# A decoder layer on one core: the attention gate's columns moved ahead of the recurrent branch's columns, softmax normalisation moved from ScalarE to VectorE, and two small reorderings at the start

## The chip, the cores and the metric

The kernel runs on one core of a Trainium2 chip. The metric is device time of one execution in microseconds (us). Before the change it is 998.0 us, the median of three runs that span 997.78 to 998.13 us.

A core has five engines that run side by side, each with its own queue of instructions in program order: TensorE (PE in the profile, with PEld for its weight loads), VectorE (DVE), ScalarE (ACT), GpSimd (POOL) and SyncE (SP), which here only issues DMA transfers. An instruction that waits for data holds back everything behind it on its engine.

## The reference

One layer of a hybrid decoder is computed for 512 prompt positions and for 8 samples of 4 positions each (544 columns in all, model width 1024):

```python
def _mixer(h, ...):
    proj = h @ w_in
    xr, q, k, v, g = jnp.split(proj, [c0, c1, c2, c3], axis=-1)
    g_lru, g_attn = jnp.split(g, 2, axis=-1)
    xc, conv_state = _causal_dwconv(xr, lru_conv_prev, conv_w, conv_b)      # width 4
    lru_out, h_last = _rg_lru(xc, lru_h0, wr, br, wi, bi, lam, pos0)        # gates from xc, then a scan
    ...                                                                     # windowed attention, softmax with a sink
    merged = jax.nn.sigmoid(g_lru) * (lru_out @ w_lru_o) + jax.nn.sigmoid(g_attn) * (attn @ w_attn_o)
    return merged @ w_out, ...
```

and then `x + RMSNorm(m)` and a feed-forward part with a width-3 convolution. The softmax is `p = exp(s - m)`, `p / (sum(p) + exp(sink - m))`. All inputs and outputs are float32.

## The kernel before, in words

**Layout.** Activations lie transposed: 128 channels on the partitions, the 544 positions along the free axis. They are worked in two halves, `a = 0` (256 columns) and `a = 1` (288 columns: 256 prompt and 32 sample positions). Every float32 operand is split into a high and a low part (`H` and `L`), and each product is three matmuls: high by high, high by low, low by high. Splitting a weight is a ScalarE copy (line 281, `wh`) and a VectorE subtraction (line 288, `wl`); splitting an activation is the same pair at lines 700 and 703, 817 and 818, 839 and 840, 957 and 958.

**Steps and ticks.** The mixer is a series of steps (`step`, line 342). A step multiplies one 128-column block of a weight by one half of the activations: 24 matmuls into one PSUM tile, of which there are three (`PM`). After step s comes tick s+1 (`tick`, line 194), which writes further work into the queues of the engines, always in this order: the high splits of the weight unit that is claimed (ScalarE); the list `late`, which holds the treatment of the result of step s-1 (from tick 8 on it comes before the side work); the side work that is due (`sides`); the list `after`; the low splits of the claimed unit (VectorE); the list `last`. One weight unit (half of a column block) is claimed at each tick, two columns ahead (`look=2`), or one ahead (`look=1`) from tick 51 on, when the gate weights `wg` hold a third of the split buffers.

**Order of the steps** (`order`, line 234; loops at lines 1062 to 1108). Steps 0 to 9 make five column blocks of q, k and v, first halves and then second halves. Steps 10 to 23 make the other seven q, k, v blocks. Steps 24 to 39 make the eight blocks of the recurrent branch (`xr`, columns 0 to 7), steps 40 to 55 the eight blocks of the attention gate (`ga`, columns 28 to 35), steps 56 to 71 the attention's output projection (`ao`), steps 72 to 87 the recurrent gate (`gl`), and then follow the projections `lo` and `out` and the feed-forward part.

**Treatment of a result.** A gate block costs VectorE one multiplication per half by the norm factors `rep` (`scaled`, line 705). A recurrent block costs one for the first half and two for the second (`xr_done`, lines 934, 938, 939), then a ScalarE pass that starts the convolution (line 942) and, from the list `after`, three VectorE passes over all 568 columns (`xr_taps`, line 951).

**Side work**, by the tick at which it is due. Sixteen attention units (a pair of heads, 128 queries) start at the ticks in `ATTN`; each takes one tick per stage: scores `psc` on TensorE; softmax on VectorE and exponentials on ScalarE (`softmax_a`); sum, reciprocal and normalisation (`softmax_b`, line 775, where the normalisation is a ScalarE multiplication put into `after`, line 779); transposes `pt`; split of the transposes; the product with v, `pvp`; and, for every second unit, the split of the result (`aH`, `aL`, one pair of instructions per head that take turns on one PSUM tile). The last units start at ticks 36, 39, 42 and 45. The samples' attention (`sample_attn`, line 859) comes in two groups. Group 0 has scores `pss` at tick 42, softmax at 43, normalisation at 44, transposes `pst` at 45, at tick 46 a VectorE copy of them (`spt`, lines 901 and 902) and at once the product `pso` that reads the copy, then copy, transpose and, at tick 49, eight pairs of tiny splits that take turns on ScalarE and VectorE (lines 920 and 921). Group 1 is five ticks later (`spt` and `pso` at tick 51, the eight pairs at 54). The recurrent gates (`gates`, line 955) of blocks 0 to 3 start at ticks 51, 53, 55 and 57: split of `xc` (`xcH` on ScalarE, `xcL` on VectorE); a tick later 12 matmuls `pg`; a tick later four sigmoids on ScalarE; a tick later a VectorE multiplication (line 979). Their exponentials follow from tick 58. The attention gate's own sigmoids (line 1085) run at ticks 52 to 58.

**The start.** The first column block is made while x is still being transposed. `turn_a(0)` and `turn_a(1)` (line 465) transpose the first and the second half of the channels of positions 0 to 255; ScalarE and VectorE split them (`hsplit`, line 449: `hH`, `hL`), and the loop at line 479 issues the first block's matmuls channel by channel. For the second and third column blocks the eight matmuls with the low weights come last (`mmhalf_low_last`, line 321), since the low weights are late there.

Of the kernel before, what the change touches and what calls it, by code (L numbers as in the profile page):

```python
# [13 lines left out]
AF = mybir.ActivationFunctionType  # L14
ALU = mybir.AluOpType
# [56 lines left out]
FIRST = 5  # L72
# [6 lines left out]
GATES = (51, 53, 55, 57, 73, 74, 75, 76)  # L79
# [44 lines left out]
def hawk_step(ctx, tc, I, O):  # L124
    nc = tc.nc
    act, dve, pool, pe = nc.scalar, nc.vector, nc.gpsimd, nc.tensor
# [25 lines left out]
    def PM(name):  # L152
        return psm.tile([P, 512], F32, tag="mm", name=name)

    def PX(name):
        return psx.tile([P, 512], F32, tag="aux", name=name)
# [7 lines left out]
    def mm(out, l, r, start, stop):  # L164
        pe.matmul(out, l, r, start=start, stop=stop)  # L165
# [7 lines left out]
    def add(out, a, b):  # L173
        dve.tensor_tensor(out=out, in0=a, in1=b, op=ALU.add)  # L174
# [6 lines left out]
    side, now, serial, late, last, mids, after = [], [0], [0], [], [], [], []  # L181

    def start_at(t, gen):
        serial[0] += 1
        side.append([t, serial[0], gen])

    def sides():
        for e in sorted((e for e in side if e[0] <= now[0]), key=lambda e: e[:2]):
            try:
                e[0] = now[0] + (next(e[2]) or 1)  # L190
            except StopIteration:
                side.remove(e)

    def tick(target=0, dt=1):
        now[0] += dt
        todo = late[:]
        late.clear()
        split = [wsplit_hi(u) for u in wclaim(target)]
        parts_ = [sides, lambda: [f() for f in todo]]
        for f in parts_ if now[0] < TURNED else parts_[::-1]:  # L200
            f()
        for f in after:
            f()
        after.clear()
        for u in split:
            wsplit_lo(*u)
        for f in last:
            f()
        last.clear()
# [23 lines left out]

    qkv_order = (16, 18, 8, 9, 10, 11, 17, 19, 12, 13, 14, 15)
    order = [("in", c) for c in qkv_order]
    order += [("in", c) for c in range(8)]
    order += [("in", 28 + c) for c in range(5)] + [("wg", 0)] + [("in", 28 + c) for c in range(5, 8)]
    order += [("ao", c) for c in range(8)] + [("wg", 1)]
    order += [("in", 20 + c) for c in range(8)]
    order += [("lo", c) for c in range(8)]  # L240
# [3 lines left out]
    wraw, wunits, wnext = {}, {}, [0]  # L244
# [42 lines left out]
    def wsplit_lo(raw, hl, eng=None):  # L287
        (eng or dve).tensor_tensor(out=hl[1], in0=raw, in1=f32(hl[0]), op=ALU.subtract)  # L288

    def upto(key, a, look):  # L290
        return 2 * (wpos[key] + look) + a + 1
# [29 lines left out]
    def mmhalf_low_last(ps, key, X, a):  # L321
        wh, wl = ([wunits[2 * wpos[key] + k // 4][j][:, k % 4, :] for k in range(KD)] for j in range(2))
        n = X.half[a][1] - X.half[a][0]
        for k in range(KD):
            mm(ps[:, :n], wh[k], X.get(k, a, 0), k == 0, False)
            mm(ps[:, :n], wh[k], X.get(k, a, 1), False, False)
        for f in mids:
            f()
        mids.clear()
        for k in range(KD):  # L330
            mm(ps[:, :n], wl[k], X.get(k, a, 0), False, k == KD - 1)

    def mmhalf(ps, key, X, a, ks=range(KD)):
        n = X.half[a][1] - X.half[a][0]
        for k in ks:
            wh, wl = (wunits[2 * wpos[key] + k // 4][j][:, k % 4, :] for j in range(2))
            xh, xl = X.get(k, a, 0), X.get(k, a, 1)
            mm(ps[:, :n], wh, xh, k == 0, False)
            mm(ps[:, :n], wh, xl, False, False)
            mm(ps[:, :n], wl, xh, False, k == KD - 1)  # L340

    def step(key, X, a, done, target=None, look=2, quick=False):

        first_ = key == order[0] and a == 0
        ps = first_ps if first_ else PM("pm" + "_".join(str(z) for z in key) + f"_{a}")
        if first_:
            pass
        elif quick:
            mmhalf(ps, key, X, a, range(4))
            now[0] += 0.5  # L350
            sides()
            mmhalf(ps, key, X, a, range(4, 8))
            done(a, ps)
        elif len(wunits) <= 2 * FIRST and a == 0 and key in order[1:3]:
            mmhalf_low_last(ps, key, X, a)
        else:
            mmhalf(ps, key, X, a)
        tick(upto(key, a, look) if target is None else target, 0.5 if quick else 1)
        if first_:
            after.append(lambda: mids.insert(1, lambda: done(a, ps)))  # L360
        elif not quick:
            (last if len(wunits) <= 2 * FIRST and a == 0 else late).append(lambda: done(a, ps))
# [59 lines left out]
    h = Full("h")  # L422
# [22 lines left out]
    def xtile(i, k):  # L445
        n = TOK[i][1]
        return xt[i, k // 4][:n, (k % 4) * P:(k % 4 + 1) * P]

    def hsplit(k, a, ps):
        g = pv[:, G_PRE + k:G_PRE + k + 1]  # L450
        act.activation(h.get(k, a, 0), ps, AF.Copy, scale=g)
        stt(h.get(k, a, 1), ps, g, f32(h.get(k, a, 0)), ALU.mult, ALU.subtract)
# [7 lines left out]
    def first_mm(k, i0, i1, start=False, stop=False):  # L460
        mm(first_ps[:, :256], wunits[k // 4][i0][:, k % 4, :], h.get(k, 0, i1), start, stop)
# [3 lines left out]
    def turn_a(z):  # L465
        for kk in (2 * z, 2 * z + 1):
            ps_ta.append(PX(f"ps_ta{kk}"))
            for q in range(4):
                pe.transpose(ps_ta[-1][:, q * P:(q + 1) * P], xtile(q % 2, 2 * kk + q // 2), ident)

    def first_low(z):
        for k in range(4 * z, 4 * z + 4):
            first_mm(k, 1, 0, stop=k == KD - 1)
# [5 lines left out]
    for q, k in enumerate(ks):  # L479
        if q in (0, 4):  # L480
            raw, hl = wsplit_hi((u0, u1)[q // 4], eng=dve)
        hsplit(k, 0, ps_ta[k // 2][:, k % 2 * 256:k % 2 * 256 + 256])
        if q in (0, 4):
            wsplit_lo(raw, hl, eng=pool)
        first_mm(k, 0, 0, start=q == 0)
        if q not in (0, 4):
            first_mm(ks[q - 1], 0, 1)
        if q == 3:
            first_mm(k, 0, 1)
            first_low(0)  # L490
            turn_a(1)
    first_mm(ks[-1], 0, 1)
    first_low(1)
    xsquare(1, 1, False)
# [280 lines left out]
    def softmax_b(s3, nh, sm, ex):  # L775
        add(sm, sm, ex)
        dve.reciprocal(sm, sm)
        for j in range(nh):
            after.append(lambda j=j: act.activation(s3[:, j, :], s3[:, j, :], AF.Copy, scale=sm[:, j:j + 1]))

    def scale_qs():
        r = rep[:, SEQ:NT].rearrange("p (b t) -> p b t", b=DB)
# [145 lines left out]
    def xr_done(c, a, ps):  # L928
        if a == 0:
            xr = xrt[c] = T(f"xr{c}")  # L930
            pool.memset(xr[:, 0:3], 0.0)
            pool.tensor_copy(xr[:, SEQ + 3:SEQ + 3 + 7 * DB].rearrange("p (b i) -> p b i", b=DB)[:, :, 0:3],
                             stT[:, c, 0:24].rearrange("p (b i) -> p b i", b=DB))
            scaled(xr[:, 3:259], ps, 0)
            return
        xr = xrt[c]
        smpv = xr[:, SEQ + 3:SEQ + 3 + 7 * DB].rearrange("p (b i) -> p b i", b=DB)
        mul(xr[:, 259:515], ps[:, 0:256], rep[:, 256:512])
        mul(smpv[:, :, 3:7], ps[:, 256:288].rearrange("p (b t) -> p b t", b=DB),
            rep[:, SEQ:NT].rearrange("p (b t) -> p b t", b=DB))  # L940
        xc[c] = S(f"xc{c}")
        act.activation(xc[c][:, 0:FLAT], xr[:, 0:FLAT], AF.Identity, bias=pv[:, C_B + c:C_B + c + 1],  # L942
                       scale=pv[:, C_W + c:C_W + c + 1])
        after.append(lambda: xr_taps(c))
# [84 lines left out]
    def once(f, *args):  # L1029
        f(*args)  # L1030
        yield
# [34 lines left out]
    for c in qkv_order[FIRST:]:  # L1066
        for a in range(2):
            step(("in", c), h, a, in_done(c))
    for c in range(8):
        for a in range(2):  # L1070
            step(("in", c), h, a, lambda a, ps, c=c: xr_done(c, a, ps))
    sg, gl = {}, {}

    def gate_done(dst, c, name, raw):
        def f(a, ps):
            lo, hi = HALF[a]
            if a == 0:
                dst[c] = S(f"{name}{c}")
            scaled(dst[c][:, lo:hi], ps, a)
            if a == 1 and not raw:  # L1080
                start_at(now[0] + 1, once(gate_later, dst, c))
        return f
# [3 lines left out]


    for c in range(8):
        raw = 42 + 2 * c < GATES[0] + 1
        for a in range(2):  # L1090
            step(("in", 28 + c), h, a, gate_done(sg, c, "ga", raw), look=1 if now[0] + 1 >= GATES[0] else 2)
        if raw:
            start_at(GATES[0] + c + 1, once(gate_later, sg, c))

    def ao_done(c):
        def f(a, ps):
# [7 lines left out]
    for c in range(8):  # L1104
        raw = 75 + 2 * c > GATES[7] + 1 and c < 7
# [651 lines left out]
    for i, x in enumerate(plan):  # L1757
# [7 lines left out]
        else:  # L1765
            _, q, c, a = x
# [132 lines left out]
    for i, kk in ((0, 0), (0, 1), (1, 0)):  # L1899
        ps = tokens(i, kk)  # L1900
# [68 lines left out]
```

## Time and profile before

| | |
|---|---|
| median of three runs | 998.0 us |
| profiled execution | 998.22 us, of which the span of instructions is 996.4 us |
| TensorE busy | 985.4 us (99%) |
| TensorE weight loads busy | 973.1 us (98%) |
| VectorE busy | 738.5 us (74%) |
| ScalarE busy | 580.4 us (58%) |
| GpSimd busy | 159.2 us (16%) |
| granted TensorE clock | 0.999 |

The times of the profile are counted from the start of the span. In rows by order of time, the first number is when an instruction starts and the second how long it takes; in square brackets stands how long the engine had been idle before it, and what ended that. Instructions of one engine overlap a little at their ends, so the cost of an instruction in a full queue is the distance to the start of the next one.

### The profile page before, as it was taken

Reading aid. Unit: us, or ns where it says so; the run is one execution under the profiler, and the core shown is the slowest. Engines: PE = TensorE matmul, PEld = TensorE weight load, DVE = VectorE, ACT = ScalarE, POOL = GpSimd, SP = SyncE. Lnnn points to the kernel's source line nnn. Section 1 sums busy time; section 2 is a strip of 40 time slices with the busy share of each in tenths; the row PEclk is TensorE's granted clock in tenths of the full one; section 3 lists DMA queues with packets and bytes.
Section 4 is the critical chain, followed back from the end, with each engine's and each line's share of the span. In section 5 each row is a group of like instructions: output and inputs, shape, how many; then the busy total and the mean of one; then the engine's idle time right before and its main releaser. Section 6 shows DMA issues by size and latency. Waiting matters only on the chain.

```text
span 996.4 us, 20115 instructions
## 1 busy us (share of the span) xinstructions
PE 985.4 (99%) x7783; PEld 973.1 (98%) x7783; DVE 738.5 (74%) x1575; ACT 580.4 (58%) x1396; POOL 159.2 (16%) x269
## 2 busy tenths in 40 slices
PE   9999999999999999999999999999999999999997
PEld 8999998999999999999999999999999999999996
DVE  5765778755846755589777788888888888888765
ACT  5655544459558534456776656565655565556652
POOL 2162000000504442210001111111010101011004
PEclk9999999999999999999999999999999999999999
DMA  7765223322333435326146767676767676768612
GB/s 209 190 223 157 68 72 93 107 86 80 93 91 98 156 114 146 86 88 207 54 117 142 176 137 181 140 180 141 176 145 173 148 170 149 170 141 208 196 45 90
DMA packets 210999, 135.62 MB, mean 136 GB/s; under 512 B 8845, under 2 KB 197021, under 8 KB 210872
## 3 DMA queue, kind: packets, MB, share of 16 engines
q1 hardware_dynamic: 198920, 112.72, 39.6%
q0 software_dynamic: 11920, 19.59, 11.9%
q10 hardware_dynamic: 64, 2.04, 0.6%
q8 instruction: 61, 1.00, 0.4%
q14 instruction: 34, 0.28, 0.1%
HBM read 111.78 MB, written 11.37 MB: 124 GB/s over the span
## 4 chain that ended last, share of the span: by engine, by line
PE 86%; DVE 8%; ACT 4%; issue 1%; DMA 1%; SPq 0%; DVEq 0%; POOL 0%; ACTq 0%
PE pmdn L165 17%; PE pux L1518 16%; PE pmin L165 14%; PE puy L1518 8%; PE pq L1518 6%; PE pmout L165 5%; PE pmao L165 5%; PE pmlo L165 5%; PE puz L1518 4%; DVE xc L177 2%; PE pg L165 1%; DVE wl_in L288 1%; PE ptok L165 1%; ACT xc L942 1%; DVE st L766 1%
## 5 line engine op out<-in xcount | busy, mean ns | idle before, releaser
L165 PE MATMUL pmin<-hH,wh_in 128*128 128x256 f32 (+1 forms) x568 | 165.7, 293 | 0.0
L165 PE MATMUL pmin<-hL,wh_in 128*128 128x256 f32 (+1 forms) x568 | 163.3, 289 | 0.0
L165 PE MATMUL pmin<-hH,wl_in 128*128 128x256 f32 (+1 forms) x568 | 161.1, 288 | 0.2 <-DVE wl_in L288 0.2
L165 PE MATMUL pmdn<-fH,wh_dn 128*128 128x256 f32 (+1 forms) x448 | 129.2, 288 | 0.2 <-DVE ft L174 0.2
L165 PE MATMUL pmdn<-fH,wl_dn 128*128 128x256 f32 (+1 forms) x448 | 129.0, 288 | 0.0
L165 PE MATMUL pmdn<-fL,wh_dn 128*128 128x256 f32 (+1 forms) x448 | 128.9, 288 | 0.0
L177 DVE SCALAR_TENSOR_TENSOR uc<-u,fv,uc 128x560 f32<-128x560 f32 x128 | 102.0, 797 | 13.3 <-ACT uc L1549 13.2
L165 PEld LDWEIGHTS pmin<-hH,wh_in 128*128 128x128 f32 x568 | 106.8, 188 | 1.4 <-issue 0.8
L165 PEld LDWEIGHTS pmin<-hL,wh_in 128*128 128x128 f32 x568 | 107.1, 189 | 0.1
L165 PEld LDWEIGHTS pmin<-hH,wl_in 128*128 128x128 f32 x568 | 106.0, 188 | 0.6 <-DVE wl_in L288 0.4
L165 PEld LDWEIGHTS pmdn<-fH,wh_dn 128*128 128x128 f32 x448 | 84.2, 188 | 0.5 <-issue 0.5
L165 PEld LDWEIGHTS pmdn<-fL,wh_dn 128*128 128x128 f32 x448 | 84.3, 188 | 0.0
L165 PEld LDWEIGHTS pmdn<-fH,wl_dn 128*128 128x128 f32 x448 | 84.2, 188 | 0.0
L1644 ACT COPY u<-pux 128x272 f32<-128x272 f32 x52 | 20.1, 386 | 83.3 <-PE pux L1518 83.3
L168 DVE TENSOR_TENSOR u<-puy,u 128x240 f32<-128x240 f32 (+2 forms) x78 | 24.6, 344 | 48.9 <-PE puy L1518 32.2
L174 DVE TENSOR_TENSOR ft<-ft,pmdn 128x256 f32<-128x256 f32 (+1 forms) x104 | 45.2, 435 | 16.6 <-PE pmdn L165 16.1
L281 ACT ACTIVATE wh_in<-raw_in 128x512 fp32r<-128x512 f32 x70 | 42.3, 623 | 12.9 <-PE pmao L165 5.1
L1549 ACT ACTIVATE uc<-u,fv 128x560 f32<-128x560 f32 x64 | 48.2, 755 | 0.0
L288 DVE TENSOR_TENSOR wl_in<-raw_in,wh_in 128x512 fp32r<-128x512 f32 x70 | 47.0, 682 | 1.3 <-ACT wh_in L281 1.3
L771 ACT ACTIVATE s<-s,st 128x256 f32<-128x256 f32 (+1 forms) x32 | 15.2, 475 | 40.7 <-DVE st L768 38.3
L1444 POOL DMA_DIRECT2D raw_up_s<-raw_up_s x26 | 22.7, 872 | 101.3 <-DMA raw_up_s<-raw_up__10513 4.5
L168 DVE TENSOR_TENSOR wl_dn<-raw_dn,wh_dn 128x512 fp32r<-128x512 f32 x56 | 38.3, 684 | 0.0
(779 smaller groups left out, 3423.4 us busy)
## 6 DMA issues: line engine op xcount, KB each, us to landing
raw_in<-in_w_in_dram SPq DMA_DIRECT2D x35, 512.0 KB
raw_dn<-in_w_down_dram SPq DMA_DIRECT2D x56, 256.0 KB
raw_up_s<-in_w_up_dram SPq DMA_DIRECT2D x25, 512.0 KB
raw_up_s<-raw_up_s POOLq DMA_DIRECT2D x26, 256.0 KB, 5.7
raw_ao<-in_w_attn_o_dram SPq DMA_DIRECT2D x8, 512.0 KB
raw_lo<-in_w_lru_o_dram SPq DMA_DIRECT2D x8, 512.0 KB
raw_out<-in_w_out_dram SPq DMA_DIRECT2D x8, 512.0 KB
xdram<-xn POOLq DMA_DIRECT2D x8, 272.0 KB, 12.1
```

The costliest lines, as they stand in the source:

```text
L165: pe.matmul(out, l, r, start=start, stop=stop)
L168: dve.tensor_tensor(out=out, in0=a, in1=b, op=ALU.subtract)
L174: dve.tensor_tensor(out=out, in0=a, in1=b, op=ALU.add)
L177: dve.scalar_tensor_tensor(out=out, in0=a, scalar=s_, in1=b, op0=op0, op1=op1)
L281: act.activation(hl[0], raw, AF.Copy)
L288: (eng or dve).tensor_tensor(out=hl[1], in0=raw, in1=f32(hl[0]), op=ALU.subtract)
L766: dve.tensor_reduce(mx, s3, AX.X, ALU.max)
L771: act.activation(s3[:, j, :], s3[:, j, :], AF.Exp, bias=ng[:, j:j + 1], accum_out=sm[:, j:j + 1])
L1444: pool.dma_start(out=w["p4"], in_=w["p2"], accum_op=ALU.add)
L1518: pe.matmul(ps[:, :HN], w, x, start=start and k == 0 and i == 0, stop=stop and k == 3 and i == 2, skip_group_check=True)
L1549: act.activation(yt[j][:, 0:FLATU], u[:, 0:FLATU], AF.Copy, scale=fv[:, j:j + 1])
L1644: act.copy(e[nm_], z)
```

## The change

1. The two loops over the column blocks change places: steps 24 to 39 now make the attention gate's blocks 28 to 35 (`ga`), steps 40 to 55 the recurrent blocks 0 to 7 (`xr`). The weight order changes with them; the gate weights `wg` keep their place in it, and `look` changes from 2 to 1 at the same tick as before.
2. The sigmoids of all eight gate blocks are due at ticks 52 to 59, one each. Before, they were due at ticks 52 to 58, two of them at 54 and two at 56.
3. The softmax normalisation is a VectorE multiplication by a per-partition factor, written into the queue right behind the reciprocal, and no longer a ScalarE multiplication in the list `after`.
4. `turn_a(1)` is issued before the fourth channel's matmuls of the first column block, and no longer behind the first four channels' low-weight matmuls.
5. The low weights come last in the fourth and fifth column blocks too.

```diff
-    order += [("in", c) for c in range(8)]
-    order += [("in", 28 + c) for c in range(5)] + [("wg", 0)] + [("in", 28 + c) for c in range(5, 8)]
+    order += [("in", 28 + c) for c in range(8)]
+    order += [("in", c) for c in range(5)] + [("wg", 0)] + [("in", c) for c in range(5, 8)]
...
-        elif len(wunits) <= 2 * FIRST and a == 0 and key in order[1:3]:
+        elif len(wunits) <= 2 * FIRST and a == 0 and key in order[1:FIRST]:
             mmhalf_low_last(ps, key, X, a)
...
+        if q == 2:
+            turn_a(1)
         if q == 3:
             first_mm(k, 0, 1)
             first_low(0)
-            turn_a(1)
...
         for j in range(nh):
-            after.append(lambda j=j: act.activation(s3[:, j, :], s3[:, j, :], AF.Copy, scale=sm[:, j:j + 1]))
+            dve.tensor_scalar(s3[:, j, :], s3[:, j, :], sm[:, j:j + 1], None, ALU.mult)
...
-    for c in range(8):
-        for a in range(2):
-            step(("in", c), h, a, lambda a, ps, c=c: xr_done(c, a, ps))
...
     for c in range(8):
-        raw = 42 + 2 * c < GATES[0] + 1
         for a in range(2):
-            step(("in", 28 + c), h, a, gate_done(sg, c, "ga", raw), look=1 if now[0] + 1 >= GATES[0] else 2)
-        if raw:
-            start_at(GATES[0] + c + 1, once(gate_later, sg, c))
+            step(("in", 28 + c), h, a, gate_done(sg, c, "ga", True))
+        start_at(GATES[0] + c + 1, once(gate_later, sg, c))
+    for c in range(8):
+        for a in range(2):
+            step(("in", c), h, a, lambda a, ps, c=c: xr_done(c, a, ps), look=1 if now[0] + 1 >= GATES[0] else 2)
```

## The prediction

> **What bounds the kernel now.** I read the page's busy times first, then the list of who waited for whom on TensorE, then the stretches in which the moved steps lie.
>
> ```profile
> PE 985.4 (99%) x7783; PEld 973.1 (98%) x7783; DVE 738.5 (74%) x1575; ACT 580.4 (58%) x1396; POOL 159.2 (16%) x269
> ```
> ```profile
> PE pt L814 <- ACT s L779: 2.1, 2, 1.3
> ```
> ```profile
> 106.07:173.24 67.17, 65.76 (x528) 65.01 (x527) 51.93 (x129) 32.18 (x83) 3.96 (x30) 1.00 0.25 75
> 173.24:235.02 61.78, 61.00 (x513) 58.75 (x512) 37.59 (x99) 37.33 (x93) 0.00 (x0) 1.00 0.34 99
> ```
>
> TensorE is the bound, with little idle: the edits can win only its waits, and every wait that they add counts in full. The two windows are the steps 24 to 41 and 42 to 55 (length, then busy time of PE, PEld, DVE, ACT, POOL). VectorE is busy 77% of the first, where the recurrent blocks stand today, and 61% of the second. Only the first has TensorE waits, two transposes that wait for ScalarE's normalisation.
>
> **Part 1: the start (edits 4 and 5).** The chain of waits at the start, and the one matmul that waits for low weights:
>
> ```profile
> 8.17 0.91 PE pm_first L165 x4
> ...
> 9.96 0.45 PE ps_ta L469 x4
> 10.44 0.48 ACT hH L451
> ```
> ```profile
> 20.49 0.28 PE L165 MATMUL pmin<-hL,wh_in 128*128 128x256 f32 x1
> 20.99 0.39 PE L165 MATMUL pmin<-hH,wl_in 128*128 128x256 f32 x1 [0.22 <-DVE wl_in L288]
> ```
>
> ScalarE's second round of splits starts at 10.44, when the first bank of the second transposes is done. After the move these transposes begin behind the third channel's matmuls, at about 8.5, and the bank is done 0.45 later, at 9.0: 1.4 earlier. The displaced matmuls fill TensorE meanwhile, and the chain of splits behind `hH` moves with the transposes. When the second half of x lands no row shows; the bounds are 0 and 1.4, and I take 1.4 since nothing waits for x at 9.96. With the low weights last, the fourth block's first low-weight matmul comes eight channels later and the 0.5 between the two rows shrinks to the usual 0.1: 0.4, and 0.5 with the slower issue behind it (bounds 0.2 and 0.7). The fifth block does not wait today: nothing. Sum: **-1.9** (0 to -2.1). The cover is that all later work is paced by TensorE.
>
> **Part 2: the first block of steps (24 to 39).** VectorE loses eight convolutions there (2.4 each, below), so normalisation is never late. The two waits go: 1.3 and 0.7 by their rows, and the slower transposes behind them, together **-2.5** (bounds 2.1 and 2.7). The normalisation itself, as VectorE work, no row shows; the nearest, in the next fence, are the gate multiplication (0.74 for 568 columns, in proportion 0.33 for 256), the `spt` copy of 256 columns (0.42) and an addition of two columns (0.15). For 256 columns I take 0.30, near the first, with the others as bounds. In this block it hides below TensorE; in the next it counts.
>
> **Part 3: the second block (40 to 55).** VectorE's queue there today, in order of time:
>
> ```profile
> 172.74 2.50 DVE L177 SCALAR_TENSOR_TENSOR xc<-xr,pv,xc 128x568 f32<-128x568 f32 x3 [0.92 <-ACT xc L942]
> 175.16 0.69 DVE L288 TENSOR_TENSOR wl_in<-raw_in,wh_in 128x512 fp32r<-128x512 f32 x1
> ...
> 177.06 0.68 DVE L168 TENSOR_TENSOR tL<-pt,tH 128x512 fp32r<-128x512 f32 x1
> 177.66 0.74 DVE L177 SCALAR_TENSOR_TENSOR s<-psc,rq,btab 128x512 f32<-128x512 f32 x1
> ...
> 179.50 0.48 DVE L177 SCALAR_TENSOR_TENSOR ss<-pss,biasS 128x320 f32<-128x320 f32 x1
> ...
> 180.87 0.69 DVE L288 TENSOR_TENSOR wl_in<-raw_in,wh_in 128x512 fp32r<-128x512 f32 x1
> 181.47 0.42 DVE L171 TENSOR_TENSOR ga<-pmin,rep 128x256 f32<-128x256 f32 x1
> 181.81 0.15 DVE L174 TENSOR_TENSOR st<-st 128x2 f32<-128x2 f32 x1
> ...
> 182.08 0.14 DVE L174 TENSOR_TENSOR st_smp<-st_smp 128x1 f32<-128x1 f32 x1
> ...
> 189.82 0.42 DVE L901 COPY spt<-pst 128x256 f32<-128x256 f32 x1
> ...
> 190.35 0.67 DVE L288 TENSOR_TENSOR wl_in<-raw_in,wh_in 128x512 fp32r<-128x512 f32 x1
> ...
> 202.42 0.17 DVE L168 TENSOR_TENSOR aL<-psot,aH 128x16 fp32r<-128x16 f32 x1
> ...
> 205.47 0.15 DVE L174 TENSOR_TENSOR st_smp<-st_smp 128x1 f32<-128x1 f32 x1
> ...
> 223.33 0.74 DVE L171 TENSOR_TENSOR xc<-ig,xc 128x568 f32<-128x568 f32 x1
> 223.99 0.68 DVE L288 TENSOR_TENSOR wl_in<-raw_in,wh_in 128x512 fp32r<-128x512 f32 x1
> ```
>
> From the distances of starts: convolution passes 2.42, low split 0.60, `tL` 0.60, softmax of a unit 1.84, of a sample group 1.37, half-block scaling 0.34, sum and reciprocal 0.27, `spt` 0.53, eight pairs 3.05, gate multiplication 0.66. A recurrent block's second half is two scalings, 0.51. The waits in the same stretch (total, times, longest), ScalarE's rows, and the matmuls to be fed:
>
> ```profile
> DVE xcL L168 <- ACT xcH L957: 6.3, 3, 2.2
> ...
> DVE aL L168 <- ACT aH L920: 3.5, 14, 0.3
> ...
> DVE aL L168 <- ACT aH L839: 2.3, 4, 1.1
> ...
> DVE tL L168 <- ACT tH L817: 1.3, 2, 0.6
> ```
> ```profile
> 171.86 0.85 ACT L942 ACTIVATE xc<-xr,pv 128x568 f32<-128x568 f32 x1
> ...
> 175.41 0.58 ACT L817 ACTIVATE tH<-pt 128x512 fp32r<-128x512 f32 x1
> ...
> 215.94 0.89 ACT L977 ACTIVATE rg<-pg,pv 128x284 f32<-128x284 f32 x2 [1.45 <-PE pg L165]
> ...
> 217.50 0.67 ACT L957 ACTIVATE xcH<-xc 128x568 fp32r<-128x568 f32 x1
> ...
> 234.65 1.28 ACT L985 ACT_TABLE_LOAD   x1
> 235.94 0.77 ACT L985 ACTIVATE rg<-rg,cneg 128x568 f32<-128x568 f32 x1
> ```
> ```profile
> 191.82 0.99 PE pso L165 x18
> 192.81 3.06 PE pmin L165 x24
> ...
> 211.12 0.99 PE pso L165 x18
> ...
> 215.51 1.56 PE pg L165 x12
> 217.07 2.83 PE pmin L165 x24
> ...
> 220.00 3.21 PE pmin L165 x24
> ```
>
> First a count. VectorE's 37.6 there lose 1.9 of a convolution that is under way at 173.24 and gain eight convolutions (19.4), 1.1 of scaling and 1.9 of normalisation (two units of two heads, two sample groups): 58.1. The four waits for ScalarE (13.4) are not free room, as the queue is in order: 71.5 against TensorE's 61.1. Some 5 may run over the end (the low weights that close the window today are needed about 5 later), so TensorE loses at least 5.4.
>
> Then the queue, place by place. Time 0 is the end of step 41 (173.24), when the first recurrent block's second half is ready.
> - Tick 43: scaling 0.5; ScalarE's `xc` (0.75) now stands ahead of its `tH` (0.58), so `tL` starts at 1.9 and ends at 2.5; both softmaxes, 5.7; passes, 8.1; low split, 8.7. Tick 44: 0.34 + 0.27 + 0.6 + 0.27 + 0.33 + 0.6, to 11.1. Tick 45: scaling and `xc`, 12.4; the two `aH`/`aL` pairs 1.6, 14.0; passes and low split, 17.0. Tick 46: 0.34 + 0.60 + 1.84 + 0.53: `spt` ends at **20.3**. TensorE reaches `pso` today at 18.5, without the transposes' wait at 17.4: it waits **2.9**. Behind `pso` stand all later matmuls.
> - `pso` ends at 21.3. Tick 47 ends at 25.5, tick 48 at 27.8 by the same prices. Tick 49 starts with step 47's end, 29.1: scaling, `xc`, `tH` and `tL` to 31.5, eight pairs to 34.8, normalisation 35.4, passes and low split 38.4. Tick 50 to 39.3; tick 51: 2.9 and `spt`, **42.7**. TensorE wants the second `pso` at 39.6: **3.1**.
> - From tick 51 weights are claimed one column ahead only. Tick 53's `xc` waits for a late VectorE; the four gate sigmoids (1.56) and `xcH` (0.67) queue behind it on ScalarE, and VectorE's `xcL`, passes and low split behind these. Tick 54, with its eight pairs, ends at 59.6; step 54 needs its low weights at 57.7, by 2.83 and 3.2 a step and 1.56 a gate block behind the second `pso`: **1.9**. For the next two blocks this loop takes 0.51 + 2.98 + 0.66 + 2.42 + 0.60 + (0.34 + 0.66 + 0.60) = 8.8, TensorE 2.83 + 3.2 + 1.57 = 7.6: twice 1.2, **2.4**.
> - Step 60 needs a split that ScalarE makes 12.6 after the last `xcH` (three attention-gate sigmoids, three weight splits, two tanh and two exponentials with four table loads of 1.29, four gate sigmoids); TensorE gets there 11.3 after it, the subtraction takes 0.7: **2.0**.
>
> Sum of part 3: **+12.3**; bounds 5.4, by the count, and 15, if every `xc` ahead of a `tH`, `aH` or `xcH` costs its 0.75 beside that.
>
> GpSimd's small copies move with their block and stand idle before and after; SyncE's loads keep their places, and the next raw weights are split several us after they land. The weights of a later VectorE come free later, which I cost at nothing.
>
> **Sum.** -1.9 - 2.5 + 12.3 = +7.9 on the profiled 998.22. That execution lies 0.2 above the median; on the median this is **1005.9 us**.
>
> **The rivals.**
> - **The second block has room (faster).** VectorE stands idle 61.8 - 37.6 = 24.2 there, more than the 20.5 that it gains, and TensorE has three result tiles and weights two columns ahead. If the waits for ScalarE shrink as the queue fills, nothing new waits: 998.0 - 4.4 = 993.6. It decides if the 13.4 of such waits fall below some 3. For it: 7.9 of idle time that waits for TensorE and does vanish. Against it: `spt` and `pso` stand in one tick, so a lag of VectorE by one convolution already shows. The Trainium skill, Perfetto Trace Analysis, section Identifying the Most-Contended Engine, finds the engine to optimise by occupancy, for TensorE by its weight loads; by that rule TensorE (98%) sets the time and VectorE's order would be hidden, which is this rival's time; I give it 0.11, since 61% is a mean over a queue that waits in order.
> - **Only the two `pso` wait.** If the gate loop hides (its 1.2 per block is the smallest margin), +6.0 - 4.4 gives 999.6. For it: today that loop has 2 of slack. Chance 0.18.
> - **ScalarE becomes the bound behind step 56.** A further switch of tables between gate sigmoids and exponentials, 1.3 each, for each of four exponentials: 5 more, 1011. The Trainium skill, ScalarE: Activation LUTs, section What ACT_TABLE_LOAD costs, puts a switch at about 2.66 us with a drain of 1.38 behind the load; by that the four loads ahead of step 60 would cost 5.5 more. The rows at 234.65 and 235.94 show 1.29 and no drain, so the sum goes by 1.29. Chance 0.07.
>
> **Chances and range.** My forecast has 0.64, the rivals 0.11, 0.18 and 0.07. The range 999.5 to 1009.5 holds the forecast with the bounds of its terms (12.3 less 3 and plus 3.6) and the second rival; the first and the third lie outside, 0.18. About 0.2% (2.0 us) can be told from no change: faster 0.11, within 0.09 (half the second rival), slower 0.80.
>
> **What would show it.** The transposes `pt` no longer wait; the waits of TensorE name `spt` at both `pso` (about 3 each) and low weights from step 54 on; VectorE is over 90% busy in the second block; the first second-half step starts about 1.9 earlier than today. The prediction is wrong if `spt` is done before step 45 ends, or if the second block has its eight convolutions without a wait of TensorE.

## The result and the profile after

The changed kernel takes 1008.66 us, the median of four executions (1007.64 to 1009.51), against 998.07 for the kernel before (997.78 to 998.36, four executions on the same chip). The ratio is 1.0106, with a 95% interval of 1.0088 to 1.0123: slower by 10.6 us. The profiled execution took 1007.64 us, with a span of 1005.8; that of before took 998.22. So the trace has to explain 9.4 us, and the forecast of +7.9 is read against that.

The page's busy times of the changed kernel, and then who waited for whom on TensorE (total us, times, longest):

```profile
PE 984.9 (98%) x7783; PEld 972.4 (97%) x7783; DVE 750.1 (75%) x1609; ACT 567.8 (56%) x1362; POOL 158.8 (16%) x269
```
```profile
PE pso L165 <- DVE spt L903: 4.0, 2, 2.5
PE pmin L165 <- DVE wl_in L288: 3.1, 2, 1.7
PE pmao L165 <- DVE wl_ao L288: 2.7, 4, 0.9
PE pkc L874 <- DVE aL L168: 1.1, 1, 1.1
...
PE pmao L165 <- ACT wh_ao L281: 0.8, 1, 0.8
```

TensorE's busy time is what it was (985.4 before), and the transposes `pt` no longer wait. In their place stand five groups of new waits, four of them for VectorE, whose own share of the span rose only from 74 to 75%. The two stretches of steps, as windows from the start of step 24 to the end of step 41, and from there to the end of step 56 (length, then busy PE, PEld, DVE, ACT, POOL):

```profile
104.45:169.49 65.04, 65.04 (x528) 65.04 (x528) 40.40 (x112) 23.37 (x63) 0.26 (x2) 1.00 0.30 85
169.49:239.12 69.63, 60.54 (x502) 57.64 (x500) 50.62 (x125) 32.57 (x79) 3.64 (x28) 1.00 0.25 74
```

The first window now runs without any idle time of TensorE. In the second, VectorE is busy 73% and TensorE loses 9.1 of 69.6 us. The first of these losses, with VectorE's queue beside it (start, length, in brackets the idle time before and what ended it):

```profile
184.29 0.63 PE L874 MATMUL pkc<-ident,cache_win_k 128*128 128x128 f32 x4 [1.09 <-DVE aL L168]
...
190.59 0.46 PE L165 MATMUL pso<-vnt,spt 64*128 64x128 f32 x2 [2.48 <-DVE spt L903]
```
```profile
184.06 2.49 DVE L177 SCALAR_TENSOR_TENSOR xc<-xr,pv,xc 128x568 f32<-128x568 f32 x3
...
187.41 0.68 DVE L168 TENSOR_TENSOR tL<-pt,tH 128x512 fp32r<-128x512 f32 x1
188.00 0.74 DVE L177 SCALAR_TENSOR_TENSOR s<-psc,rq,btab 128x512 f32<-128x512 f32 x1
...
190.18 0.27 DVE L903 COPY spt<-pst 64x128 f32<-64x128 f32 x1
```

VectorE does not rest for a moment between the convolution passes at 184.06 and `spt`, and TensorE has reached `pso` at 188.1. That is the queue that the prediction wrote out, tick by tick.

Where the 9.4 us lie, by the times at which the steps start in TensorE's timelines of the two kernels (a difference that grows from one step to the next is time lost between them):

| place | forecast | measured |
|---|---|---|
| start, up to step 10 | -1.9 | -1.6 |
| `pt` of steps 36, 39 and 42 | -2.5 | -3.3 |
| `pkc` ahead of step 45 | none | +1.25 |
| first `pso`, ahead of step 46 | +2.9 | +2.5 |
| step 50 and the second `pso` | +3.1 | +3.6 |
| low weights of step 54 | +1.9 | +1.7 |
| gate loop, steps 56 and 58 | +2.4 | +3.4 |
| step 60 | +2.0 | +1.6 |
| later | 0 | +0.2 |
| sum | +7.9 | +9.35 |

### The profile page after: what moved, and what is told of

Its sections match the earlier page's. It is cut to its first block, busy times and chain, and to the rows that moved or that the text cites. A ratio compares the mean times of both kernels' runs of the same rounds, so it can differ in the third digit from the quotient of the medians.

```text
span 1005.8 us, 20110 instructions
## 1 busy us (share of the span) xinstructions
PE 984.9 (98%) x7783; PEld 972.4 (97%) x7783; DVE 750.1 (75%) x1609; ACT 567.8 (56%) x1362; POOL 158.8 (16%) x269
## 4 chain that ended last, share of the span: by engine, by line
PE 88%; DVE 6%; ACT 4%; DMA 1%; issue 1%; SPq 0%; DVEq 0%; ACTq 0%
PE pmin L165 18%; PE pmdn L165 17%; PE pux L1517 15%; PE puy L1517 8%; PE pq L1517 6%; PE pmout L165 5%; PE pmlo L165 5%; PE puz L1517 4%; PE pmao L165 3%; DMA raw_in<-in_w_in_dram 1%; DVE xc L177 1%; PE psc L165 1%; PE pvp L165 1%; PE ptok L165 1%; PE pg L165 1%
## 5 line engine op out<-in xcount | busy, mean ns | idle before, releaser
L165 PE MATMUL pmin<-hH,wl_in 128*128 128x256 f32 (+1 forms) x568 | 158.9, 288 | 3.1 <-DVE wl_in L288 3.1
L165 PE MATMUL pmao<-aH,wl_ao 128*128 128x288 f32 (+1 forms) x128 | 37.4, 292 | 2.7 <-DVE wl_ao L288 2.7
```

## The experiments

The theory, A, is that of the prediction: the convolution's passes overfill VectorE's queue where the samples' attention and the gate loop need it. The rivals are told with each run. Unless a run is said to be a single execution, its ratio goes against the kernel before on the same chip.

### The parts of the change alone

The block order alone (edits 1 and 2), the normalisation alone (edit 3), the start alone (edits 4 and 5), and edits 3 to 5 without the new order. Each is the kernel before with just those hunks of the diff, for instance for the second:

```diff
-            after.append(lambda j=j: act.activation(s3[:, j, :], s3[:, j, :], AF.Copy, scale=sm[:, j:j + 1]))
+            dve.tensor_scalar(s3[:, j, :], s3[:, j, :], sm[:, j:j + 1], None, ALU.mult)
```

> Only the order of the blocks and the due times of the gate sigmoids change (edits 1 and 2). Theory A, VectorE's queue in steps 40 to 55: the new waits of TensorE in steps 44 to 61 belong to the order. In the changed kernel they add up to 14.2 us; without the normalisation VectorE has 1.9 less to do there, so 12 to 14 stay; the waits of steps 36 to 42, up to 3.3 us, go all the same, since VectorE is light there. That makes +9 to +11 on 998.1, about 1008. Rival B, the normalisation overfills VectorE and the order alone is nearly free: +3 or less, under 1001.5.

> Only the normalisation moves to VectorE (edit 3), in the old order of the blocks. Theory A: the waits of the transposes for ScalarE at steps 36 to 42 (2.1 us by name, 3.3 with the slower issue behind them) go in part, because VectorE is 77% busy there and gains about 4 us: -1 to -2, 996 to 997. Rival B: VectorE is too full there too, and the time stays or grows, 998 or more. Rival C: all of it is won, 994.8.

> Only the two reorderings at the start (edits 4 and 5). In the changed kernel step 5 begins 1.54 us earlier than before and step 10 1.60 earlier, and no wait before step 36 takes that back. If the gain is carried to the end, as theory A says because TensorE paces everything behind it: 998.1 - 1.6 = 996.5. Rival: a later wait that is fixed to a transfer takes it back, 998.

> Edits 3, 4 and 5 without the new order of the blocks. Theory A: the gains of the two runs with these edits alone add up, about -1.6 and -1 to -2, so 994.5 to 995.5, faster than both kernels. If the edits need the new order to work, 997 to 998.

Measured, against 998.01 for the kernel before (997.25 to 998.39):

| kernel | median us (lowest to highest) | ratio (95%) |
|---|---|---|
| order alone | 1011.34 (1009.24 to 1013.21) | 1.0130 (1.0114 to 1.0145) |
| normalisation alone | 997.00 (996.31 to 998.58) | 0.9993 (0.9985 to 1.0002) |
| start alone | 996.07 (995.51 to 996.50) | 0.9982 (0.9974 to 0.9991) |
| normalisation and start | 995.39 (994.49 to 996.68) | 0.9975 (0.9966 to 0.9985) |

The order alone is the whole loss; rival B of the first run (the normalisation overfills VectorE) is out. Its median lies some 3 us above A's forecast. In its profiled execution (1012.63 us) the steps after 42 lose 17.5 us, of which 4.4 are no wait but a lower clock, told in the last section; the remaining 13.1 are in A's 12 to 14. Since the changed kernel loses 14.25 in the same stretch, the normalisation on VectorE costs it about 1.1 there, by one execution of each, more than half of it at `pkc` (1.25 against 0.65). The start gains 1.9, as the prediction had it (the run's own forecast was 1.6), and the gain is carried to the end. Normalisation and start together gain 2.6, inside the 994.5 to 995.5 of that run's A. What the normalisation gains is not settled by its own run, whose interval holds 1.

Two of the waits for the normalisation do go there, but a third grows. TensorE's and VectorE's timelines of the kernel with the normalisation alone, at step 39:

```profile
161.64 0.53 PE L814 MATMUL pt<-ident,s 128*128 128x128 f32 x2 [1.76 <-DVE s L779]
```
```profile
157.57 2.50 DVE L177 SCALAR_TENSOR_TENSOR xc<-xr,pv,xc 128x568 f32<-128x568 f32 x3
...
161.30 0.48 DVE L779 TENSOR_SCALAR s<-s,st 128x128 f32<-128x128 f32 x2
```

The reciprocal (161.10) stands behind a convolution, and so the multiplication is late, on VectorE as it was on ScalarE before. The waits of steps 36 and 42 (0.4 and 1.2) go, that of step 39 grows by 0.3.

### Without the passes

The changed kernel, with the loop over the three passes in `xr_taps` taken out:

```diff
-        for t in range(1, 4):
-            wv = pv[:, C_W + 8 * t + c:C_W + 8 * t + c + 1]
-            stt(xc[c][:, 0:FLAT], xr[:, t:t + FLAT], wv, xc[c][:, 0:FLAT], ALU.mult, ALU.add)
```

> The changed kernel without the three VectorE passes of the convolution (the convolution's result is left out; ScalarE's pass stays). It takes about 2.5 us per block from VectorE and nothing from ScalarE. Theory A, the passes in VectorE's queue make TensorE's new waits: of the 14.2 us that steps 43 to 66 lose, at least 12 go, so 994 to 997. Rival B, ScalarE's queue makes them (its pass ahead of the other work, the four sigmoids, the table loads of the gates): the waits at steps 54 to 61, about 6.7, stay, so 1001 or more.

One execution: 996.25 us, 12.4 below the changed kernel's median and 11.4 below its profiled execution. TensorE's list of waits, its rows at this place:

```profile
PE pso L165 <- DVE spt L903: 1.1, 1, 1.1
...
PE pmao L165 <- ACT wh_ao L281: 0.9, 1, 0.9
...
PE pmao L165 <- DVE wl_ao L288: 0.2, 1, 0.2
```

Of the 14.2 us some 11 are gone, and what stays is one `pso` and step 60, where ScalarE's weight split is late. A holds in the main, though it forecast that at least 12 would go; rival B (ScalarE's queue) keeps 1.7 us at step 60, not 6.7.

### The samples earlier

The changed kernel with the samples' attention twelve ticks earlier, its last splits held back, since their destination does not exist earlier:

```diff
-SAMPLE = (41, 46)
+SAMPLE = (29, 34)
...
         dve.tensor_copy(so, po[:, 0:HD])
-        yield
+        yield 13
```

> The changed kernel with the samples' attention up to the product pso twelve ticks earlier (ticks 29 and 34, where VectorE is 64% busy), its last splits where they were. Theory A: the two waits for spt (2.5 and 3.6 us with the slower issue behind) and the 1.2 at pkc go, and VectorE's queue in steps 40 to 55 loses some 5 us, so the low-weight wait at step 54 (1.7) goes too; the gate loop's waits at steps 56 to 61 (5.0) stay: about 1000 to 1002. Rival B, VectorE is short of time in steps 40 to 55 whatever it does first: the waits move to other readers (pt, pvp, low weights) and less than 4 us are won, 1005 or more.

One execution: 1006.78 us, only 1.9 below the changed kernel's median and 0.9 below its profiled execution. The waits moved to another reader, as rival B has it. Up to step 50 all went as A has it, and the steps start 2.9 us earlier than in the changed kernel. Then the low split of the next weights is late instead. TensorE's row, VectorE's queue, and two windows around it (the column of 1.00 and 0.57 is the granted clock):

```profile
208.64 0.39 PE L165 MATMUL pmin<-hH,wl_in 128*128 128x256 f32 x1 [4.26 <-DVE wl_in L288]
```
```profile
202.42 0.16 DVE L168 TENSOR_TENSOR aL<-psot,aH 128x16 fp32r<-128x16 f32 x1
...
205.48 2.50 DVE L177 SCALAR_TENSOR_TENSOR xc<-xr,pv,xc 128x568 f32<-128x568 f32 x3
207.90 0.68 DVE L288 TENSOR_TENSOR wl_in<-raw_in,wh_in 128x512 fp32r<-128x512 f32 x1
```
```profile
204.40:208.60 4.20, 0.00 (x0) 0.00 (x0) 3.50 (x8) 1.50 (x5) 0.00 (x0) 1.00 0.00 0
208.60:212.60 4.00, 3.96 (x20) 3.96 (x21) 2.20 (x6) 2.06 (x5) 0.51 (x4) 0.57 0.40 119
```

In tick 49 the eight pairs (3.05 us of taking turns) and a convolution (2.4) stand ahead of the low split. Not all of the loss is waiting: by the starts of the steps, the lower clock behind this wait, and behind a second one of 2.19 us in step 54, added some 3 us. Without it the kernel would stand at about 1004, between the forecasts of A (1002 at most) and B (1005 at least), so the run shows B's mechanism, but B's time only with the clock's help. While `pso` waited for VectorE, this lag was hidden behind that wait; with `pso` on time it shows in full. Removing one reader's wait hands the lag to the next reader in the queue.

### The gates later

The changed kernel with the gates of blocks 0 to 3, their exponentials and scans four ticks later:

```diff
-GATES = (51, 53, 55, 57, 73, 74, 75, 76)
-EXPS = (58, 59, 60, 61, 78, 79, 80, 81)
-SCANS = (62, 63, 65, 67, 82, 83, 85, 86)
+GATES = (55, 57, 59, 61, 73, 74, 75, 76)
+EXPS = (62, 63, 64, 65, 78, 79, 80, 81)
+SCANS = (66, 67, 69, 71, 82, 83, 85, 86)
```

> The changed kernel with the recurrent gates of blocks 0 to 3, their exponentials and scans four ticks later; the attention gate's sigmoids and the claiming of weights stay. Theory A: the waits before step 52 (1.2, 2.5 and 3.6) stay; of the 6.7 at steps 54 to 61 the part that comes from the loop xc, sigmoids, xcH, xcL, passes, low split goes, at least 4: 1002 to 1005. Rival B: those waits come from VectorE's lag alone and stay: 1007 to 1009.

One execution: 1002.46 us, 6.2 below the changed kernel's median and 5.2 below its profiled execution. The waits for `wl_ao` and `wh_ao` are gone; those for `pkc`, `spt` and low weights at steps 50 and 54 stay:

```profile
PE pso L165 <- DVE spt L903: 4.1, 2, 2.5
PE pmin L165 <- DVE wl_in L288: 2.6, 2, 1.7
PE pm_first L165 <- DVE wh_in L283: 1.1, 1, 1.1
PE pkc L874 <- DVE aL L168: 1.1, 1, 1.1
```

So most of the losses from step 55 on come from the loop of `xc`, sigmoids, `xcH`, `xcL`, passes and low split, as A has it.

### Other orders of the blocks

First, gate and recurrent blocks in turns, with and without the later gates:

```diff
+    pairs = [("in", z + c) for c in range(8) for z in (28, 0)]
+    order += pairs[:13] + [("wg", 0)] + pairs[13:]
```

> The changed kernel with the sixteen blocks in turns, one gate block and one recurrent block, so that each half of the stretch has four convolutions. Theory A: VectorE's 91 us of work over the two blocks (104.45 to 239.12 us) lie evenly, at 70% of TensorE's 126; neither the waits of the old order (3.3) nor those of the new one come: 998.1 - 1.6 - 3.3 = 993.2, up to 995 if some of the late waits stay. Rival B: a single convolution ahead of spt or of a low split is enough for a wait: 997 to 1001.

> The alternating order together with the recurrent gates of blocks 0 to 3, their exponentials and scans four ticks later. In the alternating kernel TensorE waits 0.65 for spt, 1.86 for a low split behind the eight pairs and a convolution (206.08), 0.34 for spt, 1.36 for a low split (225.68) and about 1.2 behind ScalarE's gates (247 on). Theory A: the last two come from the gate loop and go, the first three stay: 998.6 - 2.5 = 996.0. Rival B: the later gates only push the waits to later steps: 998 or more.

In turns: 998.57 us (998.26 to 998.85), ratio 1.0006 (0.9997 to 1.0015) to 998.1; with the later gates 997.24 (996.85 to 998.16), ratio 0.9994 (0.9985 to 1.0002) to 998.11. The first is 3.6 us above the upper end of A's forecast and fits rival B: half the convolutions suffice for waits. The second lies between A's 996.0 and B's 998. TensorE's list of the kernel in turns:

```profile
PE pmin L165 <- DVE wl_in L288: 2.9, 2, 1.7
...
PE pso L165 <- DVE spt L903: 0.7, 2, 0.5
```

The rows behind it are at 206.08, where tick 49 has the eight pairs and a convolution again, and at 225.68, where tick 54's pairs follow a convolution in the gate loop. The load is even, but convolutions still stand in the wrong ticks. The later gates gain 1.3, not the 2.5 expected: the 1.2 from step 60 on goes, and of the 1.4 at step 54 1.1 stays.

Then an order that keeps the convolutions out of ticks 46, 49 and 54:

```diff
+MIXED = (0, 1, 2, 28, 3, 29, 4, 30, 5, 31, 6, 32, 7, 33, 34, 35)
...
+    pairs = [("in", c) for c in MIXED]
+    order += pairs[:13] + [("wg", 0)] + pairs[13:]
```

> The changed kernel with the recurrent blocks at places 0, 1, 2, 4, 6, 8, 10, 12 of the sixteen and the gate blocks between and behind them; the gates at their old ticks. Convolutions then fall into ticks 27, 29, 31, 35, 39, 43, 47 and 51, none into tick 46 (spt), 49 or 54 (eight pairs), and one at most beside the gate loop. Theory A, a wait comes where a convolution stands in VectorE's queue ahead of spt, the pairs' low split or the gate loop: TensorE waits less than 1.5 in steps 24 to 61, so 998.1 - 1.6 - 3.3 + 1 = 994.2 (993 to 995). Rival B, VectorE's total counts and not the places: as the alternating order, 998 or more.

> The mixed order with the gates of blocks 0 to 3 four ticks later. No convolution runs beside the gates any more in either. Theory A: the same as the mixed order within 0.7, 993 to 995, since the loop has no convolution in it that could be late. Rival B: the attention gate's sigmoids and the table loads between them and the exponentials (1.29 each) still hold ScalarE's weight splits at steps 60 and 61, and the later gates win 1 or more.

> The mixed order with the softmax normalisation back on ScalarE (edit 3 undone). It tells what the normalisation on VectorE is worth where VectorE has room. Theory A: the reciprocal of VectorE is early enough in this order, so that ScalarE's multiplication is early too: the same as the mixed order within 0.5, 993 to 993.6. Rival B: the multiplication in the list behind the treatment of results is late by itself, and the waits of the transposes at steps 36 to 42 come back: 995 to 996.5.

Against 998.11: the mixed order 993.09 us (992.93 to 993.69), ratio 0.9952 (0.9938 to 0.9965); with later gates 993.14, ratio 0.9951 (0.9938 to 0.9963); with the normalisation back on ScalarE 993.00, ratio 0.9951 (0.9937 to 0.9965). All of TensorE's waits in steps 24 to 61 of the mixed order, and two windows that hold both blocks:

```profile
PE pso L166 <- DVE spt L904: 0.3, 1, 0.3
```
```profile
104.00:165.00 61.00, 61.00 (x497) 61.00 (x497) 49.67 (x129) 24.99 (x66) 2.60 (x20) 1.00 0.26 73
165.00:228.00 63.00, 62.68 (x527) 60.75 (x527) 43.28 (x113) 33.38 (x84) 1.37 (x10) 1.00 0.37 106
```

VectorE does 81% in the first window and 69% in the second, 93 us in all, and TensorE hardly waits. About the same VectorE work (91 us in the changed kernel's two windows) cost 14 us there and 5 in turns. So its total over both blocks does not decide, nor an even share; the places do. One thing is not parted from the places: ticks 42 to 57 hold three convolutions in the mixed order, against four in turns and eight in the changed kernel. The mixed order beats both kernels, and with it neither the later gates nor edit 3 makes a difference, as A forecast for both runs.

## Why the prediction was right, and where it was off

**The count and its verdict.** The forecast of slower, +7.9 us on the profiled execution, became +9.4 there and +10.6 in the medians; 1008.66 lies inside the range of 999.5 to 1009.5, near its upper end. The first rival (the second block has room) would have needed VectorE's waits for ScalarE to fall from 13.4 to below some 3. VectorE's list of waits in steps 42 to 56 of the changed kernel:

```profile
DVE xcL L168 <- ACT xcH L958: 6.2, 2, 3.1
DVE aL L168 <- ACT aH L921: 3.5, 14, 0.3
DVE aL L168 <- ACT aH L840: 3.4, 4, 1.3
DVE xr L171 <- PE pmin L165: 3.3, 2, 2.5
DVE tL L168 <- ACT tH L818: 2.9, 2, 1.5
DVE xc L177 <- ACT xc L943: 0.8, 1, 0.8
```

The four kinds that it counted grew to 16.0, and with the wait for ScalarE's `xc` to 16.8. So most of the 19 us in which VectorE stands idle there is no room, because the queue is in order. The waits for `tH` and `aH` (line 840) grew by 1.6 and 1.1; that ScalarE's `xc`, itself released by VectorE, stands ahead of them is read from the order of the queues and was not tried by itself.

Two of the prediction's signs did not come as written. VectorE was to be over 90% busy in the second block and was 73% busy: the count's 58.1 us of VectorE work, of which some 5 were let run over the end, came out as 50.6. The lag comes from a queue with waits in it rather than from too much work, and it was the tick-by-tick queue that carried the forecast, not the count. And low weights are late from step 50 on, not from step 54. The prediction's second window, called steps 42 to 55, ends with step 56, which runs from 232.19, and of the two waiting transposes one stands in it, at 174.11, and not in the first; neither changes the sum.

The Trainium skill, Perfetto Trace Analysis, section Identifying the Most-Contended Engine, would look first at the engine of highest occupancy, here TensorE at 97% of weight loads; the run without the passes shows that VectorE, busy 75% of the span, set some 11 us.

**Part 1, -1.9 forecast, -1.6 in the changed kernel.** The two terms hold: the second block starts 1.3 earlier (1.4 forecast), and steps 3 to 4 gain another 0.5 (0.5 forecast). What is lacking is due to the transfer of the fourth block's weights, which the forecast did not name. The changed kernel's chain of waits:

```profile
11.63 6.83 DMA raw_in<-in_w_in_dram
...
18.48 0.64 ACT wh_in L281
...
19.17 3.11 PE pmin L165 x24
```

Step 3 starts when its weights have landed and are split, and is 1.1 earlier instead of 1.4; 1.1 and 0.5 are the 1.6. The gain follows this landing from trace to trace: 18.04 and a gain of 2.05 by step 24 in the mixed order, 18.09 and 2.00 with normalisation and start, 18.46 and 1.62 here, 18.73 and 1.37 with the start alone, whose median still gained 1.9.

**Part 2, -2.5 forecast, -3.3 measured.** Both named waits and a third, smaller one at step 36 go. The forecast took only the two that the list names; the size was off, the mechanism right. The gain belongs to the order, which takes the convolutions away, as the prediction put it: the order alone, with the multiplication on ScalarE, starts step 42 earlier by 3.3 as well.

**Part 3, +12.3 forecast, +14.25 measured.** `spt` was ready 20.9 us after step 41 (20.3 forecast) and the second one 43.9 after it (42.7 forecast). Three terms were mis-sized. The queue table did not look at the transposes `pkc`, whose PSUM tile is freed by `aL`; VectorE's lag holds them up for 1.25 ahead of step 45, and that shortens the wait at `pso`. The wait "TensorE wants the second `pso` at 39.6: 3.1" came as two, 1.7 for step 50's low weights and 1.6 for `spt`, because the eight pairs and a convolution share tick 49; the total was 3.6. And the gate loop cost 3.4 instead of 2.4: its two turns came at 1.0 to 1.3 each, as forecast, and a further 0.9 stands at 248.87, where a VectorE multiplication took twice its time beside one of GpSimd:

```profile
246.63 1.58 DVE L171 TENSOR_TENSOR xc<-ig,xc 128x568 f32<-128x568 f32 x1
```
```profile
246.48 1.13 POOL L988 TENSOR_TENSOR lt<-rg 128x568 f32<-128x568 f32 x1 [6.67 <-ACT rg L986]
```
```profile
248.87 0.38 PE L165 MATMUL pmao<-aH,wl_ao 128*128 128x256 f32 x1 [0.75 <-DVE wl_ao L288]
```

Step 60's term, ScalarE's splits behind sigmoids, exponentials and table loads, got 1.6 instead of 2.0.

**What normalisation costs in the second block** was taken as 1.9 of VectorE's time. The multiplication itself came as priced: 0.62 for two of 256 columns (0.60 forecast).

```profile
179.24 0.62 DVE L780 TENSOR_SCALAR s<-s,st 128x256 f32<-128x256 f32 x2
```

The losses there grew by about 1.1, as the traces with and without it show when the lower clock is left out; the rest went into time that VectorE spent in waits. With the convolutions spread, it is worth nothing either way.

## What to carry to other kernels

An engine that is busy 60 or 70% can still set the end if its queue is in order: write down what stands ahead of each result that the bound engine needs, tick by tick, and compare the times at which both arrive; the mean and even an equal share of work in two halves say little. A wait that is removed hands the lag to the next reader unless the work ahead of it is moved, so move the heavy instruction (here a convolution of 2.4 us) out of the few ticks in which short, urgent work must pass. Before pricing an edit by the engine that does it, ask whose lateness it waits for: the normalisation was late on both engines, because the reciprocal ahead of it was.

## What the runs showed of the hardware beside that

The multiplication `xc<-ig,xc` takes 0.74 us alone; 0.15 us behind the start of GpSimd's `lt<-rg` (1.13 us) it took 1.58, and the same in the kernel with the order alone (1.59, beside a `lt<-rg` that starts 0.15 earlier). In the kernel before, the two did not meet. The Trainium skill, SBUF — State Buffer, section SBUF: two separate sides, has a VectorE operation with two inputs in SBUF wait for the whole of a GpSimd instruction that started first; the rows agree: 246.48 + 1.13 = 247.61, and the multiplication ends 0.60 after that. A shift of a few us is enough to bring such a pair together.

After a wait of TensorE the granted clock sometimes falls. In the profiled execution of the order alone, the wait for `spt` lasted 2.48 us, as it does in the changed kernel, but the clock stood at 0.50 behind it:

```profile
191.61 0.76 PE L165 MATMUL pso<-vnt,spt 64*128 64x128 f32 x2 [2.48 <-DVE spt L902]
```
```profile
191.60:193.40 1.80, 1.79 (x19) 1.16 (x19) 1.13 (x5) 1.80 (x6) 0.52 (x4) 0.50 0.03 9
193.40:196.00 2.60, 2.60 (x12) 2.60 (x13) 1.89 (x3) 2.25 (x5) 0.00 (x0) 0.50 0.87 250
196.00:198.60 2.60, 2.60 (x16) 2.60 (x15) 1.44 (x4) 0.00 (x0) 0.00 (x0) 0.60 0.52 153
198.60:203.40 4.80, 4.80 (x42) 4.32 (x41) 2.38 (x7) 1.27 (x4) 0.00 (x0) 1.00 0.01 4
```

Step 46 took 5.16 us instead of 3.04, the first `pso` ahead of it 1.71 instead of 0.97, and step 51, behind the second `pso`, 4.92 instead of 3.40: 4.4 us that no queue explains, and that account for nearly all of the 4.6 us by which this execution lies above the forecast of about 1008. The Trainium skill, TensorE: Matmul & The Clock Gate, section What's actually happening, puts the clock at half after about 3.4 us without work. Here 2.48 us was enough in one kernel and not in the other, and 4.26 us in the run with the samples earlier gave 0.57 for 4 us. A shorter wait did it too: with normalisation and start together, the wait of 1.76 us at step 39 was followed by a clock of 0.56 for 3.84 us, which cost 1.5 us; with the normalisation alone the same wait left the clock at 1.00. The four executions of the changed kernel fit this: 1007.64 and 1007.96 us at a mean granted clock of 0.998, 1009.51 and 1009.36 at 0.997 and 0.996. That such a fall makes the last two longer, and with them the 1.0 us between the profiled time and the median, is argued from their clocks; there is no trace of them. A new wait of some 1.7 us or more on TensorE should so be priced with up to 3 us of slow clock behind it (2.1 and 0.7 behind the first `pso` here), which may or may not come.
